# Block pairs in another product order: two products accumulate onto a tile that one ScalarE copy took

## The chip, the cores and the metric

One core of a Trainium2 chip runs the kernel. The metric is the time of one execution on the device in microseconds (us), the median of several runs. TensorE multiplies (PE in the profile), VectorE (DVE) and ScalarE (ACT) do elementwise work, GpSimd (POOL) issues the accumulating DMAs, SyncE (SP) the loads.

## The reference

One layer of a streaming encoder on 576 tokens (512 of a prompt and 64 of a running stream), 1024 channels, all in fp32:

```python
def encoder_layer(x, ...):
    x = x + 0.5 * swiglu_ffn(rms_norm(x, ffn1_norm), ffn1_w_gate_up, ffn1_w_down)
    h = rms_norm(x, mix_norm)
    p = h @ w_in
    ...
    y_b = b_act @ w_b_out
    merged = jax.nn.sigmoid(gate_a) * y_a + jax.nn.sigmoid(gate_b) * y_b
    x = x + merged @ w_out
    x = x + 0.5 * swiglu_ffn(rms_norm(x, ffn2_norm), ffn2_w_gate_up, ffn2_w_down)
    return x, ...

def swiglu_ffn(x, w_gate_up, w_down):
    gate, up = jnp.split(x @ w_gate_up, 2, axis=-1)
    return (jax.nn.silu(gate) * up) @ w_down
```

The hidden width of both FFNs is 2816, which is 22 tiles of 128.

## The kernel before

**Exact products.** Activations and weights are split into a high part, rounded to fp32r, and a low part, the rest. A product is three matmuls: high by high, high by low, low by high. Activations lie with channels on partitions and tokens in the free direction, 576 tokens as two halves of H = 288.

**Block pairs.** Where two output tiles (an FFN's gate and up tile of one index i) read the same activations, the kernel works on a 2 x 2 block form: weight blocks A11, A12, A21, A22 (two tiles by two halves of the 1024 channels) against activation blocks (two halves of channels by two halves of tokens). Instead of eight block products it takes seven, by sums: weight sums s1 = a21 + a22, s2 = s1 + a11, s3 = a11 + a21, s4 = s2 + a12, with signs folded into the arithmetic, and activation sums t1 to t4, made once for a phase (`Forms.operands`). The seven weight blocks of a pair are its *units* 0 to 6, the seven products are numbered in the same way. A product is 12 matmuls (4 tiles of channels by 3) of 128 x 128 weights with 288 columns, and fills one bank of PSUM. PSUM has four tiles of two banks each (`mmps`); `bank()` hands out one bank at a time. There are 41 such pairs: FFN1 i = 4 to 21, FFN2 i = 1 to 21, and two in branch B's output projection (`block_pair`).

**Combining.** In `pair`, after each product a step runs that takes the products so far into `t` (the gate's tile, both halves) and `cu` (the up tile): ScalarE copies product 0 out of PSUM (288 columns), VectorE does six additions up to the end of `gate`, where `t` is multiplied by R (the norm's reciprocal root) and ScalarE takes its Silu. A seventh addition comes later in `up`. `up`, `hidden` (the product of the two, and its high part by ScalarE) and `parts` (the low part) are appended to `rest` and run behind the first products of the next pair, one a product. In the last group of each FFN, `up` holds another multiply by R (`if last`).

**The weight stream.** `Stream` (`ws`) loads raw weights by SyncE and prepares units ahead of their use: `add` makes the sums on VectorE, `begin` casts the high part on ScalarE, `end` subtracts for the low part on VectorE. For units that are raw weights the low part is instead made by ScalarE (times -1) and an accumulating DMA that GpSimd issues (`how == "dma"`). `get(n)` leads the stream on to six units past n (`AHEAD_UNITS`), so the fetch for one product casts a unit that is used a pair later, roughly.

**Order.** Each engine runs its instructions in the order in which the code issues them (`Ordered`). In a pair, the fetch `ws.get(...)` for product n comes ahead of its matmuls, and the step on product n - 1 behind them; so the gate of a pair is issued behind the fetch for product 6. Pairs run in groups of hidden tiles (`GROUPS`: 0 to 4, 5 to 9, 10 to 15, 16 to 21). After each group follow the down products of the group: two output tiles at a time for j = 0, 1 (`both`), then one by one.

Of the kernel before, what the change touches and what calls it, by code (L numbers as in the profile page):

```python
# [13 lines left out]
ALU = mybir.AluOpType  # L14
# [8 lines left out]
KU = KT // 2  # L23
T = SEQ + DSEQ
H = T // 2
# [86 lines left out]
def tile_encoder_step(  # L112
# [237 lines left out]
    def plan_block(name, raws, homes, low="dma"):  # L350

        a21, a22, a11, a12 = raws
        s1, s2, s3, s4 = ((name, n) for n in range(1, 5))
        plan[name] = [
            ws.unit(src, KU, home, how, sums)
            for home, (src, how, sums) in zip(homes, (
                (a11, low, ((s1, (a21, a22)),)),
                (s2, "dve", ((s2, (s1, a11)),)),
                (s1, "dve", ()),
                (s3, "dve", ((s3, (a11, a21)),)),  # L360
                (a12, low, ()),
                (s4, "dve", ((s4, (s2, a12)),)),
                (a22, low, ()),
            ))
        ]
        ws.second.update(plan[name][n] for n in (1, 5, 6))

    def plan_ffn(f, gu, dn):
        for g, grp in enumerate(GROUPS):
# [79 lines left out]
            got += [(w, kk) for kk in range(ws.units[n][1])]  # L449
        return got  # L450

    def block(w, xs):

        q = bank()[:, :H]
        for k in range(KU):
            (whi, wlo), (xh, xl) = w, xs[k]
            for m, (l, r) in enumerate(((whi, xh), (whi, xl), (wlo, xh))):
                pe.matmul(q, l[:, k, :], r, start=k == m == 0, stop=k == KU - 1 and m == 2)
        return q


    work = []
# [180 lines left out]
    class Forms:  # L643
# [25 lines left out]
        def operands(self, xg):  # L669

            first, second = (
                [(half(hi, s), half(lo, s)) for hi, lo in xg] for s in range(2)
            )
            t1, t2, t3, t4 = (
                [(half(hi, s), half(lo, s)) for hi, lo in (self.parts[p][i] for p in range(KU))]
                for i in range(2) for s in range(2)
            )
            return first[:KU], t2, t1, t3, first[KU:], second[KU:], t4


    ss = Sum()
# [138 lines left out]
    def ffn(f, xg, sums, finish, forms, R=None, todo=()):  # L820
# [40 lines left out]
                    step(p)  # L861

        def pair(i, hs, last):
            qu, uu, t, cu = (ttile() for _ in range(4))
            q1, u2, u3, u4 = half(qu, 0), half(qu, 1), half(uu, 0), half(uu, 1)
            q = []

            def q7():
                dve.tensor_tensor(u3, q[3], u2, op=ALU.add)
                dve.tensor_tensor(half(cu, 1), u3, q[2], op=ALU.subtract)  # L870
# [14 lines left out]
            for n, xs in enumerate(bs):  # L885
                q.append(block(ws.get(plan[f, "s", i][n]), xs))
                if n > 0:
                    steps[n - 1]()
                if rest:
                    rest.pop(0)()  # L890

            hs.append(None)
            at = len(hs) - 1

            def up():
                if last:
                    dve.tensor_tensor(t, t, R, op=ALU.mult)
                dve.tensor_tensor(half(cu, 0), q[6], u3, op=ALU.add)

            def hidden():  # L900
                dve.tensor_tensor(cu, cu, t, op=ALU.mult)
# [337 lines left out]

    def block_pair(i):  # L1240
        j = 2 * i
        c1, c2, qu, uu = (ttile() for _ in range(4))
        q1, u2, u3, u4 = half(qu, 0), half(qu, 1), half(uu, 0), half(uu, 1)
        q = []

        def second():
            dve.tensor_tensor(u3, q[3], u2, op=ALU.add)
            dve.tensor_tensor(half(c2, 1), u3, q[2], op=ALU.subtract)

            if i == KU - 1:  # L1250
                MS[4], MS[5] = split(M[4]), split(M[5])

        def first():
            dve.tensor_tensor(half(c1, 1), q[5], u4, op=ALU.add)
            dve.tensor_tensor(c1, c1, SGB[j], op=ALU.mult)
            merged(j, c1)

        steps = (
            lambda: sca.copy(q1, q[0]),
            lambda: dve.tensor_tensor(u2, q[1], q1, op=ALU.subtract),  # L1260
            lambda: dve.tensor_tensor(u4, q[2], u2, op=ALU.subtract),
            second,
            lambda: dve.tensor_tensor(half(c1, 0), q[4], q1, op=ALU.add),
            first,
        )
        for n, xs in enumerate(bs):
            q.append(block(ws.get(plan["yb", "s", i][n]), xs))
            if n > 0:
                steps[n - 1]()
        dve.tensor_tensor(half(c2, 0), q[6], u3, op=ALU.add)  # L1270
        dve.tensor_tensor(c2, c2, SGB[j + 1], op=ALU.mult)
        merged(j + 1, c2)
        spare.clear()
# [164 lines left out]
```

## Time and profile before

| | |
|---|---|
| runs | 1294.07, 1295.1, 1296.71 us, median 1295.1 us |
| profiled execution: span from first to last instruction | 1290.1 us |
| TensorE | 1279.4 us busy, 99%, 9728 matmuls |
| VectorE | 925.1 us, 72%, 1539 instructions |
| ScalarE | 765.5 us, 59%, 1359 instructions |
| GpSimd | 361.6 us, 28%, 460 instructions |

The profiled execution has no time of its own beside its span; the median of the runs lies 5.0 us above it. The profile gives busy time by engine, a chain of waits followed back from the last instruction, a list of what each engine waited for, and a timeline. A timeline row reads: start in us, duration, engine, line, operation, output and inputs by the program's names, shapes, count, and in brackets the idle time before it and what ended it. Neighbouring instructions of one kind are merged into one row, so that 12 matmuls of a product make one. All rows have line 88, since a helper records every operation.

### The profile page before, as it was taken

The page shows a single profiled execution, that of the slowest core. Times are in us where ns is not written, and L with a number is a line of the kernel's source. Part 1 is how long each engine was busy: PE and PEld are TensorE (multiplying, and loading weights), DVE is VectorE, ACT ScalarE, POOL GpSimd, SP SyncE. Part 2 cuts the span into 40 slices and gives each one's busy share as a digit, 9 for nine tenths or more (in the row PEclk, how much of TensorE's full clock was granted, in tenths as well). Part 3 has the DMA queues.
Part 4 walks back from the last instruction along what each step waited for, and adds up shares of the span by engine and source line. Part 5 has one row for each costly group of instructions (what it writes and reads, how often), then busy time and mean ns, then how long its engine had stood idle before and what let it go on. Part 6 is the DMA issues. An engine that isn't in the chain of part 4 may idle for free.

```text
span 1290.1 us, 25702 instructions
## 1 busy us (share of the span) xinstructions
PE 1279.4 (99%) x9728; PEld 1277.5 (99%) x9728; DVE 925.1 (72%) x1539; ACT 765.5 (59%) x1359; POOL 361.6 (28%) x460
## 2 busy tenths in 40 slices
PE   9999999999999999999999999999999999999997
PEld 9999999999999999999999999999999999999997
DVE  6868668748846998888895166656867848847956
ACT  7655646646776645555444576477665655654664
POOL 0032332232333444333321221122142141241230
PEclk9999999999999999999999999999999999999998
DMA  7286787886799898788885767696687696796783
GB/s 220 70 181 154 163 180 155 177 181 149 154 224 232 174 200 173 165 172 174 172 172 124 163 142 154 151 236 145 139 175 171 151 197 151 164 204 138 158 172 97
DMA packets 286812, 215.26 MB, mean 167 GB/s; under 512 B 15456, under 2 KB 248928, under 8 KB 286688
## 3 DMA queue, kind: packets, MB, share of 16 engines
q0 software_dynamic: 56160, 92.43, 43.3%
q1 hardware_dynamic: 228784, 120.35, 32.8%
q8 instruction: 77, 1.26, 0.4%
q10 hardware_dynamic: 1744, 0.83, 0.2%
q14 instruction: 47, 0.39, 0.1%
HBM read 116.17 MB, written 4.98 MB: 94 GB/s over the span
## 4 chain that ended last, share of the span: by engine, by line
PE 92%; issue 4%; DVE 2%; DMA 1%; ACT 1%; POOL 0%; DVEq 0%; POOLq 0%; ACTq 0%
PE mm L88 92%; DVE tmp L88 0%; DMA g<-raw 0%; DMA raw<-in_w_b_out_dram 0%; DVE x L88 0%; DVE g L88 0%; DMA u<-raw 0%; ACT act L88 0%; DVE w L88 0%; POOL u L88 0%; DVE act L88 0%; ACT u L88 0%; ACT w L88 0%; ACT g L88 0%; POOL g L88 0%
## 5 line engine op out<-in xcount | busy, mean ns | idle before, releaser
L88 PE MATMUL mm<-act,u 128*128 128x288 f32 x4758 | 668.3, 293 | 0.1
L88 PEld LDWEIGHTS mm<-act,u 128*128 128x128 f32 x4758 | 638.9, 188 | 0.4 <-DMA u<-raw 0.3
L88 PE MATMUL mm<-act,g 128*128 128x288 f32 x3030 | 432.9, 294 | 0.9 <-DMA g<-raw 0.9
L88 PEld LDWEIGHTS mm<-act,g 128*128 128x128 f32 x3030 | 410.3, 188 | 1.1 <-DMA g<-raw 1.1
L88 POOL DMA_DIRECT2D u<-raw x197 | 172.3, 874 | 481.7 <-ACT u L88 317.4
L88 PE MATMUL mm<-act,act 128*128 128x288 f32 (+2 forms) x1896 | 259.9, 293 | 0.0
L88 PEld LDWEIGHTS mm<-act,act 128*128 128x128 f32 x1896 | 252.2, 188 | 0.5 <-ACT act L88 0.3
L88 ACT CAST u<-raw 128x512 fp32r<-128x512 f32 (+2 forms) x207 | 118.8, 574 | 172.0 <-PE mm L88 136.7
L88 POOL DMA_DIRECT2D g<-raw x126 | 109.9, 872 | 297.4 <-ACT g L88 242.7
L88 DVE SCALAR_TENSOR_TENSOR w<-g,prm,w 128x606 f32<-128x606 f32 x232 | 179.3, 844 | 1.4 <-ACT w L88 1.4
L88 DVE TENSOR_TENSOR tmp<-mm,tmp 128x288 f32<-128x288 f32 (+1 forms) x251 | 112.9, 459 | 70.3 <-PE mm L88 53.7
L88 ACT ACTIVATE u<-u 128x512 fp32r<-128x512 f32 (+2 forms) x197 | 116.8, 593 | 6.2
L88 ACT CAST g<-raw 128x512 fp32r<-128x512 f32 (+2 forms) x136 | 75.1, 553 | 43.9 <-DMA raw<-in_ffn_w_down_dram 17.6
L88 DVE SCALAR_TENSOR_TENSOR tmp<-mm,r 128x576 f32<-128x576 f32 x48 | 36.3, 757 | 76.6 <-PE mm L88 76.6
L88 POOL DMA_DIRECT2D act<-raw x67 | 59.1, 883 | 108.3 <-ACT act L88 94.5
L88 ACT CAST act<-tmp 128x576 fp32r<-128x576 f32 x92 | 61.9, 675 | 43.1 <-DVE tmp L88 42.1
L88 ACT CAST g<-w 128x512 fp32r<-128x512 f32 x79 | 49.0, 620 | 64.4 <-DVE w L88 58.6
L88 ACT CAST u<-w 128x512 fp32r<-128x512 f32 x81 | 50.2, 619 | 61.0 <-DVE w L88 43.6
L88 DVE TENSOR_TENSOR act<-tmp,act 128x576 fp32r<-128x576 f32 x92 | 67.5, 754 | 18.1 <-ACT act L88 16.5
L88 ACT ACTIVATE g<-g 128x512 fp32r<-128x512 f32 (+2 forms) x126 | 72.1, 572 | 4.0
L88 DVE TENSOR_TENSOR w<-raw,raw 128x512 f32<-128x512 f32 x82 | 56.2, 685 | 16.2 <-DMA raw<-in_ffn_w_gate_up_dram 11.2
L88 ACT ACTIVATE tmp<-tmp 128x576 f32<-128x576 f32 x47 | 32.2, 686 | 45.1 <-DVE tmp L88 45.0
(86 smaller groups left out, 830.6 us busy)
## 6 DMA issues: line engine op xcount, KB each, us to landing
raw<-in_ffn_w_gate_up_dram SPq DMA_DIRECT2D x171, 256.0 KB, 3.5
u<-raw POOLq DMA_DIRECT2D x140, 256.0 KB, 4.2
raw<-in_w_in_dram SPq DMA_DIRECT2D x112, 256.0 KB, 3.8
raw<-in_ffn_w_down_dram SPq DMA_DIRECT2D x96, 192.0 KB, 3.8
g<-raw POOLq DMA_DIRECT2D x69, 256.0 KB, 4.2
act<-raw POOLq DMA_DIRECT2D x61, 256.0 KB, 4.4
g<-raw POOLq DMA_DIRECT2D x43, 192.0 KB, 4.5
u<-raw POOLq DMA_DIRECT2D x41, 192.0 KB, 4.5
```

Source lines behind the costliest of these rows:

```text
L88: return self.tc.keep_in_program_order(fn(*args, **kwargs))
```

## The change

A function `seven` takes the place of the loops in `pair` and `block_pair`. It takes two PSUM tiles of two banks (`first`, `second`) and one bank (`last`). Units 1 and 2 trade places, so that products 0 and 1 lie in the two banks of `first`, and one ScalarE copy of 576 columns takes both. Products 4 and 5 are then multiplied with `start=False` onto the same two banks, and so add up with products 0 and 1 in place. After product 3 VectorE does three additions (`middle`). After product 5, ScalarE copies bank 0 as the first half of the gate, VectorE adds for the second half, and the gate follows (`close`). The last addition (product 6) is returned as a function and runs where it ran. A pair then has five additions on VectorE where it had seven, two ScalarE copies where it had one.

```diff
                 (a11, low, ((s1, (a21, a22)),)),
-                (s2, "dve", ((s2, (s1, a11)),)),
-                (s1, "dve", ()),
+                (s1, "dve", ((s2, (s1, a11)),)),
+                (s2, "dve", ()),
                 (s3, "dve", ((s3, (a11, a21)),)),
...
-    def block(w, xs):
+    def block(w, xs, q, new):
-        q = bank()[:, :H]
...
+                pe.matmul(
+                    q, l[:, k, :], r, start=new and k == m == 0,
+                    stop=k == KU - 1 and m == 2, skip_group_check=not new,
+                )
+    def seven(ws7, xs7, c1, c2, gate, between=None):
+        qq, uu = ttile(), ttile()
+        u2, u3 = half(uu, 0), half(uu, 1)
+        first, second = psum2(), psum2()
+        q = [first[:, 0, :H], first[:, 1, :H], second[:, 0, :H], second[:, 1, :H]]
+        def middle():
+            dve.tensor_tensor(u2, q[2], half(qq, 0), op=ALU.subtract)
+            dve.tensor_tensor(u3, q[3], u2, op=ALU.add)
+            dve.tensor_tensor(half(c2, 1), u3, half(qq, 1), op=ALU.subtract)
+        def close():
+            sca.copy(half(c1, 0), q[0])
+            dve.tensor_tensor(half(c1, 1), q[1], u2, op=ALU.subtract)
+            gate()
+        steps = {
+            1: lambda: sca.copy(halves(qq), first[:, :, :H]),
+            3: middle,
+            5: close,
+        }
+        last = bank()[:, :H]
+        for n, (w, xs) in enumerate(zip(ws7, xs7)):
+            block(ws.get(w), xs, (q + q[:2] + [last])[n], n not in (4, 5))
+            if n in steps:
+                steps[n]()
+            if between:
+                between()
+        return lambda: dve.tensor_tensor(half(c2, 0), last, u3, op=ALU.add)
...
         def pair(i, hs, last):
...
             def gate():
-                dve.tensor_tensor(half(t, 1), q[5], u4, op=ALU.add)
                 dve.tensor_tensor(t, t, R, op=ALU.mult)
                 sca.activation(t, t, AF.Silu)
-            steps = (
-                lambda: sca.copy(q1, q[0]),
-                lambda: dve.tensor_tensor(u2, q[1], q1, op=ALU.subtract),
-                lambda: dve.tensor_tensor(u4, q[2], u2, op=ALU.subtract),
-                q7,
-                lambda: dve.tensor_tensor(half(t, 0), q[4], q1, op=ALU.add),
-                gate,
-            )
-            for n, xs in enumerate(bs):
-                q.append(block(ws.get(plan[f, "s", i][n]), xs))
-                if n > 0:
-                    steps[n - 1]()
+            final = seven(plan[f, "s", i], bs, t, cu, gate, between)
```

Before, the step on product 5 stood behind the fetch for product 6; now it stands ahead of it. What this does to the engines' order, at three places:

ScalarE, from the gate of a pair in the last group of FFN1. Before (`tmp_722` is the gate's tile, `g_746` the unit that the fetch for product 6 casts, which is unit 5 of the next pair; `act_762` the high part of the hidden product):

```order
L88 CAST g_746_4252<-w_744_4233 128x512 [waits DVE_49,PE_49]
L88 ACTIVATE tmp_722_4121<-tmp_722_4121 128x576 [waits DVE_49]
L88 CAST u_754_4278<-raw_701_3984 128x512 [waits DMAHW3_49,PE_49]
L88 ACTIVATE u_754_4278<-u_754_4278 128x512 [waits Activation_49]
L88 CAST g_759_4304<-raw_739_4196 128x512 [waits DMAHW0_49,PE_49]
L88 ACTIVATE g_760_4305<-g_759_4304 128x512 [waits DMASW7_49,PE_49,Activation_49]
L88 COPY tmp_749_4271<-mm_748_4255 128x288 [waits DVE_49]
L88 CAST act_762_4324<-tmp_723_4122 128x576 [waits DVE_49]
```

And after (`tmp_734` is the gate's tile, `u_759` the cast of unit 5 of the next pair, `tmp_762` the copy of the next pair's products 0 and 1):

```order
L88 COPY tmp_734_4241<-mm_738_4245 128x288 [waits PE_49]
L88 ACTIVATE tmp_734_4241<-tmp_734_4241 128x576 [waits DVE_49,Activation_49]
L88 CAST u_759_4375<-w_756_4352 128x512 [waits DMASW1_49]
L88 CAST g_768_4399<-raw_718_4110 128x512 [waits DMAHW7_49]
L88 ACTIVATE g_769_4400<-g_768_4399 128x512 [waits DMASW6_49,Activation_49]
L88 CAST u_774_4426<-raw_752_4316 128x512 [waits DMAHW4_49,DMASW2_49,PE_49]
L88 ACTIVATE u_774_4426<-u_774_4426 128x512 [waits Activation_49]
L88 COPY tmp_762_4391<-mm_764_4393 128x576 [waits PE_49]
L88 CAST act_775_4444<-tmp_735_4242 128x576 [waits DVE_49]
```

The Silu (ACTIVATE of the gate's tile, 576 columns) stood behind the cast of unit 5 of the next pair, and now stands ahead of it, behind a copy that is new; the copy of the next pair has 576 columns in place of 288.

VectorE at the same place. Before (the first three rows are the gate's last additions and its multiply by R, `g_747` the low part of unit 5 of the next pair, whose cast is `g_746`; the second multiply by R follows):

```order
L88 TENSOR_TENSOR tmp_722_4121<-mm_743_4217,tmp_720_4119 128x288 [waits PE_49]
L88 TENSOR_TENSOR tmp_722_4121<-mm_743_4217,tmp_721_4120 128x288
L88 TENSOR_TENSOR tmp_722_4121<-tmp_722_4121,r_78_421 128x576 [waits DVE_49]
L88 TENSOR_TENSOR g_747_4253<-w_744_4233,g_746_4252 128x512 [waits DMASW6_49,Activation_49]
L88 TENSOR_TENSOR w_753_4276<-raw_728_4133,raw_729_4135 128x512 [waits DMAHW7_49,DMAHW6_49]
L88 TENSOR_TENSOR tmp_722_4121<-tmp_722_4121,r_78_421 128x576 [waits Activation_49]
L88 TENSOR_TENSOR tmp_723_4122<-mm_748_4255,tmp_721_4120 128x288 [waits PE_49]
L88 TENSOR_TENSOR w_758_4302<-w_753_4276,raw_739_4196 128x512 [waits DMAHW0_49,DVE_49]
L88 TENSOR_TENSOR tmp_723_4122<-tmp_723_4122,tmp_722_4121 128x576 [waits DVE_49]
```

After (the first row is the addition for the second half of the gate, `u_759` the low part of unit 5 of the next pair):

```order
L88 TENSOR_TENSOR tmp_734_4241<-mm_738_4245,tmp_737_4244 128x288 [waits Activation_49]
L88 TENSOR_TENSOR tmp_734_4241<-tmp_734_4241,r_78_421 128x576 [waits DVE_49]
L88 TENSOR_TENSOR u_759_4375<-w_756_4352,u_759_4375 128x512 [waits DMASW1_49,Activation_49]
L88 TENSOR_TENSOR w_767_4397<-raw_743_4256,raw_744_4258 128x512 [waits DMAHW3_49,DMAHW2_49]
L88 TENSOR_TENSOR tmp_734_4241<-tmp_734_4241,r_78_421 128x576
L88 TENSOR_TENSOR tmp_735_4242<-mm_712_4097,tmp_737_4244 128x288 [waits PE_49]
L88 TENSOR_TENSOR w_773_4424<-w_767_4397,raw_752_4316 128x512 [waits DMAHW4_49,DVE_49]
L88 TENSOR_TENSOR tmp_735_4242<-tmp_735_4242,tmp_734_4241 128x576 [waits DVE_49]
L88 TENSOR_TENSOR act_778_4461<-tmp_735_4242,act_775_4444 128x576 [waits Activation_49]
```

The low part still follows the gate's multiply, but it reads a cast which ScalarE now issues behind the Silu of that multiply's result. An addition is gone.

TensorE at the first pair of FFN1, the last matmuls of product 3 and the first of product 4. Before (`mm_175` holds products 2 and 3, `mm_181` is the tile that product 4 takes):

```order
L88 MATMUL mm_175_901<-act_149_825,u_155_837 128x288
L88 MATMUL mm_175_901<-act_144_720,u_155_837 128x288
L88 MATMUL mm_181_939<-act_39_239,g_156_839 128x288 [waits PE_49,Activation_49]
L88 MATMUL mm_181_939<-act_40_240,g_156_839 128x288
L88 MATMUL mm_181_939<-act_39_239,g_157_840 128x288 [waits DVE_49]
```

After (`mm_166` holds products 2 and 3, `mm_165` products 0 and 1):

```order
L88 MATMUL mm_166_857<-act_149_825,u_155_837 128x288
L88 MATMUL mm_166_857<-act_144_720,u_155_837 128x288
L88 MATMUL mm_165_856<-act_39_239,g_156_839 128x288 [waits Activation_49]
L88 MATMUL mm_165_856<-act_40_240,g_156_839 128x288
L88 MATMUL mm_165_856<-act_39_239,g_157_840 128x288 [waits DVE_49]
```

Product 4 went to a tile of its own; it now goes onto the bank of product 0, and its first matmul waits for ScalarE, which is the copy of both banks.

More of the change, by code (lines that the diff above doesn't have):

```diff
@@ L365, in plan_block @@
         ]
-        ws.second.update(plan[name][n] for n in (1, 5, 6))
+        ws.second.update(plan[name][n] for n in (2, 5, 6))
     def plan_ffn(f, gu, dn):
@@ L1241, in block_pair, with between @@
         j = 2 * i
[L1242 to L1251, printed above, removed]
+        c1, c2 = ttile(), ttile()
         def first():
-            dve.tensor_tensor(half(c1, 1), q[5], u4, op=ALU.add)
             dve.tensor_tensor(c1, c1, SGB[j], op=ALU.mult)
             merged(j, c1)
[L1258 to L1270, printed above, removed]
+        def between():
+            if i == KU - 1 and between.n == 4:
+                MS[4], MS[5] = split(M[4]), split(M[5])
+            between.n += 1
+        between.n = 0
+        seven(plan["yb", "s", i], bs, c1, c2, first, between)()
         dve.tensor_tensor(c2, c2, SGB[j + 1], op=ALU.mult)
```

14 lines of the change are left out of this document (4 added, 10 removed).

## The prediction

> **What bounds the kernel now.** I read the page first (engine totals, then the chain), next the list of what TensorE waited for, and then the timeline of each engine over one pair of the last feed-forward group, because its queues are the fullest.
>
> ```profile
> span 1290.1 us, 25702 instructions
> PE 1279.4 (99%) x9728; PEld 1277.5 (99%) x9728; DVE 925.1 (72%) x1539; ACT 765.5 (59%) x1359; POOL 361.6 (28%) x460
> PE 92%; issue 4%; DVE 2%; DMA 1%; ACT 1%; POOL 0%; DVEq 0%; POOLq 0%; ACTq 0%
> ...
> PE mm L88 <- DMA g<-raw: 0.9, 1, 0.9
> PE mm L88 <- ACT tmp L88: 0.5, 1, 0.5
> ```
>
> TensorE is busy for 99% of the span and is 92% of the chain that ended last. After start-up it waited twice for something that this change can touch: 0.9 us for a weight's low part and 0.5 us for ScalarE. Nearly nothing can be won while TensorE keeps the same matmuls; what can be lost is any wait that reaches it. So the question is whether the new dependence (product 4 of a pair waits for a copy by ScalarE) is met in time. Products are numbered 0 to 6, weight units of a pair too, a time with a + counts from the start of product 0 of the pair, and unit 5 and product 5 of the *next* pair are written 5'.
>
> ```profile
> 1219.85 1.74 PE L88 MATMUL mm<-act,u 128*128 128x288 f32 x12
> 1226.16 1.74 PE L88 MATMUL mm<-act,u 128*128 128x288 f32 x12
> 1230.89 1.74 PE L88 MATMUL mm<-act,g 128*128 128x288 f32 x12
> 1241.94 3.33 PE L88 MATMUL mm<-act,u 128*128 128x288 f32 x24
> ```
>
> These rows of TensorE's timeline are product 0 and product 4 of a pair, product 0 of the last pair, and the first down product. A pair takes 1230.89 - 1219.85 = 11.04 us, the last one 1241.94 - 1230.89 = 11.05, a product 1.58, and product 4 starts at +6.31. The two other engines over the same pair:
>
> ```profile
> 1221.33 0.69 ACT L88 ACTIVATE tmp<-tmp 128x576 f32<-128x576 f32 x1 [1.40 <-DVE tmp L88]
> 1221.92 0.60 ACT L88 CAST u<-raw 128x512 fp32r<-128x512 f32 x1
> 1224.27 0.38 ACT L88 COPY tmp<-mm 128x288 f32<-128x288 f32 x1
> 1224.84 0.68 ACT L88 CAST act<-tmp 128x576 fp32r<-128x576 f32 x1 [0.19 <-DVE tmp L88]
> 1225.42 0.61 ACT L88 CAST u<-w 128x512 fp32r<-128x512 f32 x1
> 1225.94 0.62 ACT L88 CAST g<-w 128x512 fp32r<-128x512 f32 x1
> 1232.10 0.69 ACT L88 ACTIVATE tmp<-tmp 128x576 f32<-128x576 f32 x1 [0.86 <-DVE tmp L88]
> ...
> 1220.54 0.76 DVE L88 TENSOR_TENSOR tmp<-tmp,r 128x576 f32<-128x576 f32 x1
> 1221.21 0.69 DVE L88 TENSOR_TENSOR g<-w,g 128x512 fp32r<-128x512 f32 x1
> 1221.82 0.68 DVE L88 TENSOR_TENSOR w<-raw,raw 128x512 f32<-128x512 f32 x1
> 1222.42 0.75 DVE L88 TENSOR_TENSOR tmp<-tmp,r 128x576 f32<-128x576 f32 x1
> 1223.09 0.45 DVE L88 TENSOR_TENSOR tmp<-mm,tmp 128x288 f32<-128x288 f32 x1
> 1223.45 0.68 DVE L88 TENSOR_TENSOR w<-w,raw 128x512 f32<-128x512 f32 x1
> 1224.05 0.75 DVE L88 TENSOR_TENSOR tmp<-tmp,tmp 128x576 f32<-128x576 f32 x1
> 1225.55 0.76 DVE L88 TENSOR_TENSOR act<-tmp,act 128x576 fp32r<-128x576 f32 x1 [0.37 <-ACT act L88]
> 1226.22 0.69 DVE L88 TENSOR_TENSOR u<-w,u 128x512 fp32r<-128x512 f32 x1
> 1226.83 0.69 DVE L88 TENSOR_TENSOR w<-raw,raw 128x512 f32<-128x512 f32 x1
> 1228.39 0.45 DVE L88 TENSOR_TENSOR tmp<-mm,tmp 128x288 f32<-128x288 f32 x1
> 1228.88 0.45 DVE L88 TENSOR_TENSOR tmp<-tmp,mm 128x288 f32<-128x288 f32 x1
> 1229.25 0.68 DVE L88 TENSOR_TENSOR u<-w,u 128x512 fp32r<-128x512 f32 x1
> 1229.85 0.68 DVE L88 TENSOR_TENSOR w<-w,raw 128x512 f32<-128x512 f32 x1
> 1231.31 0.76 DVE L88 TENSOR_TENSOR tmp<-tmp,r 128x576 f32<-128x576 f32 x1
> ```
>
> The reader is to see the gate's multiply (1220.54), the Silu (1221.33), then VectorE's low part at 1221.21, which began before the Silu, since its cast was done. From multiply to multiply the loop takes 1231.31 - 1220.54 = 10.77, a little under a pair of 11.04.
>
> **The change part by part.** *Removed:* two VectorE additions in each of 41 pairs. Instructions of that kind follow each other at 1229.25 - 1228.88 = 0.37, so 82 x 0.37 = 30 us of VectorE. VectorE is 2% of the chain, so most of this buys nothing by itself.
>
> ```profile
> L88 ACT COPY tmp<-mm 128x576 f32<-128x576 f32 x8 | 5.0, 623 | 0.0
> L88 ACT COPY tmp<-mm 128x288 f32<-128x288 f32 x41 | 15.8, 384 | 9.0 <-PE mm L88 9.0
> ```
>
> *Added:* ScalarE's 41 copies grow from 0.384 to 0.623, and 41 copies of 0.384 come in: 41 x 0.239 + 41 x 0.384 = 25.5 us on an engine that is 59% busy. By itself that costs nothing either; it is covered by ScalarE's idle 41%, as long as no one waits for its place in the queue.
>
> *Moved, and this I hold to be the decisive part:* the close of a pair (copy, last addition, gate multiply, Silu) is now issued ahead of the fetch of the last unit, so on ScalarE the Silu stands before the cast of unit 5', and on VectorE the low part of unit 5' stands right behind the gate multiply. That low part needs the cast, the cast waits behind the Silu, the Silu waits for the multiply. All that VectorE has behind it (the next sums, the hidden product, whose high part is again ScalarE's, the middle step, the next close) hangs on that chain. One turn of it, by start differences of the rows above: multiply to Silu 0.79, Silu to cast 0.59, cast 0.62 and 0.03 to land: 2.03. Low 0.61, sum 0.60, second multiply by R 0.67, final addition 0.36, sum 0.60, hidden product until its cast 0.79, that cast until VectorE goes on 0.71: 6.37. Low of the activation 0.67, low 0.61, sum 0.60: 8.25. Middle step 0.49 + 0.49 + 0.37: 9.60. Two lows and a sum, 0.60 each, and the last addition 0.49 (as from 1228.39 to 1228.88): 11.89. TensorE's pair is 11.04: the chain falls behind by 0.85 us a pair, where before it gained 0.27. The second multiply by R is in the last group of each FFN alone; elsewhere the turn is 11.22, at most 0.18 behind, and five turns of that stay within the slack named next.
>
> *The new wait.* In the pair after a group's first, the Silu starts at -1.58 + 0.17 (product 5 out) + 0.41 (copy) + 0.49 + 0.79 = +0.28. From the Silu to the end of the wide copy stand on ScalarE: 0.59 (Silu), 0.52 (cast 5', 1225.42 to 1225.94), four weight casts 1224.27 - 1221.92 = 2.35, the copy 0.62 + 0.03: 4.11. So the copy ends at +4.39, and product 4 needs it at +6.31: slack 1.92. In the last group it ends at 4.39, 5.24, 6.09 in the second to fourth pair, 6.94 in the fifth (wait 0.63), and, that wait having been given back, 7.16 in the sixth (wait 0.85): 1.48 for a group. Ends: 0 if the loop keeps pace, and 5 x 0.85 = 4.3 if it had no slack; I take 1.48, which the row by row sum gives.
>
> *The down product behind it.* The accumulate DMAs of its units are issued behind the same casts.
>
> ```profile
> 1238.00 0.86 POOL L88 DMA_DIRECT2D u<-raw  x1
> ...
> u<-raw POOLq DMA_DIRECT2D x41, 192.0 KB, 4.5
> ```
>
> Before, this issue came 1238.00 - 1232.10 = 5.90 behind the Silu; with cast 5' and the wider copy ahead of it, 5.90 + 0.52 + 0.29 = 6.7. With the Silu at 7.16 - 4.11 = +3.05 in the sixth pair, and 4.5 to land, it is there at +14.26; the product that reads it would want it at 11.05 + 0.85 (the wait) + 0.80 (six matmuls of the first unit) + 0.52 (four more before its low part) = +13.2. Wait 1.05; ends 0 (before, the Silu at +1.21, it was there 0.7 ahead, so a landing 1 us quicker hides it) and 2. A last group costs 1.48 + 1.05 = 2.5, twice 5.0.
>
> *First pairs.* There the copy is late for another reason: ScalarE is still behind with casts.
>
> ```profile
> 63.17 1.74 PE L88 MATMUL mm<-act,g 128*128 128x288 f32 x12
> 914.49 1.74 PE L88 MATMUL mm<-act,g 128*128 128x288 f32 x12
> 928.91 2.08 PE L88 MATMUL mm<-act,u 128*128 128x288 f32 x12
> ...
> 63.41 0.39 ACT L88 COPY tmp<-mm 128x288 f32<-128x288 f32 x1
> 915.19 0.38 ACT L88 COPY tmp<-mm 128x288 f32<-128x288 f32 x1
> ```
>
> Product 4 of FFN1's first pair starts at 63.17, the copy that it will wait for at 63.41: 63.41 + 0.65 - 63.17 = 0.9 of wait. In FFN2's first pair: 915.19 + 0.65 - 914.49 = 1.35. That wait lets VectorE and ScalarE catch up, so the wait that before fell at 928.91 (0.5 by the list of waits) goes; the next pairs have no margin left (0.1), and the down product after that group I put at 0.6, between 0 and the 1.05 of the last group. FFN2's first group: 1.35 - 0.5 + 0.1 + 0.6 = 1.55. The other groups and the two pairs of branch B I put at 0, with 0.5 either way, by the slack of 1.92.
>
> *Sum:* 5.0 + 0.9 + 1.55 = 7.45 on the profiled span of 1290.1: 1297.5. The median of the runs shown, 1295.1, lies 5.0 above that span, so 1302.5.
>
> **A rule weighed.** The trace has the wide copy 1.92 us clear of product 4 in a pair that is not behind. The Trainium skill (Perfetto Trace Analysis, Matmuls under Optimizing Tensor Performance) says that independent matmul groups should rotate through different PSUM banks so that the evacuation of one overlaps the next group's matmuls. Here two products go back to a bank that has just been evacuated, so by that rule every pair is at risk; if each of the 41 lost the last group's mean of 1.48 / 5 = 0.3, the sum would grow to about 12 us, 1307. By the rows two other products lie between, and only a late ScalarE exposes the copy.
>
> **The rivals.** *A, no measurable change (0.2% of 1295.1 is 2.6 us, about what a measurement can tell):* the serial turn is shorter than my 11.89, because an instruction that waits on another engine is picked up sooner than the back to back rows show; from 0.85 us less a turn nothing accumulates. For it: the turn before (10.77) had 0.27 to spare. Against: 0.85 is made of whole instructions, 1.14 of Silu and cast. Then only the first pairs count: 0.9 + 1.35 - 0.5 = 1.75, 1296.9.
>
> *B, faster:* VectorE's relief is what counts. The removed 30 us are 3.3% of its 925.1; of its 2% of the chain (26 us) that is 0.85, and twice this if the additions stood where others wait; with the waits of 0.9 and 0.5 gone too, up to 3.1 us are won, 1292.0. It decides if the turn of the loop ends below 11.04 and the copies of the first pairs, too, come earlier by 0.9 and 1.35, since VectorE holds up ScalarE there. For it: 72% busy VectorE; against: the casts ahead of the copy at 63.41 wait for no VectorE. The rule that the Trainium skill gives in VectorE: DVE Perf Modes, Rules for kernel authors, to minimize the count of operations, speaks for this rival; the chain of this trace speaks against it.
>
> *C, much slower:* the lag is larger (a fifth more, 1.02 a pair), the landings under load take 5.4, and the groups without the second multiply reach the wait in their last pair as well. Then the copies of a last group cost 2.3, its down product 1.9, four other groups 0.7 each: 1290.1 + 0.9 + 1.55 + 8.4 + 2.8 + 5.0 = 1308.8.
>
> **How the numbers follow.** My forecast, slower by stalls in the last groups and the first pairs, gets 0.55, with its own range 1299.5 to 1305.5 from the ends above (down product 0 to 2 in each of two groups, 0.5 for the rest). A gets 0.20, B 0.07, C 0.12, and 0.06 go to a half lag between A and the forecast, on the slow side. Slower by over 0.2%: 0.55 + 0.12 + 0.06 = 0.73; within: 0.20; faster: 0.07. The time is that of the forecast. The range goes down to 1296.0, which takes in most of A, and up to 1308.5, just under the centre of C; outside lie B, half of C and the lower part of A, about 0.2.
>
> **What would show it.** VectorE 82 instructions fewer, ScalarE 41 more. In the list of waits, TensorE waiting for ScalarE's copy: at 63 us, at 914 us, and late in the last groups of the two FFNs, the second from 1180 to 1245 us (I hold FFN1's to be like it); in these, from pair to pair, the Silu 0.85 later against product 0, and VectorE idle before the low part of unit 5' with ScalarE as the releaser. If the Silu keeps its distance, the serial turn is wrong and A or B holds; if TensorE waits at product 4 in groups without the second multiply, C. I'm also wrong if waits fall on the down products for other transfers, or TensorE's step between matmuls changes when two products share a bank.

## The result and the profile after

The changed kernel takes 1303.05 us, the median of seven runs (1298.63 to 1304.42); the kernel before, on the same chip, 1294.64 us (1291.48 to 1296.71, seven runs). The ratio is 1.0061, 95% interval 1.004 to 1.0082: slower by 7.9 us (0.0061 of 1294.64; the two medians lie 8.4 apart), with 1302.5 forecast. A second set of six runs gave 1300.88 us and the ratio 1.0063 (1.004 to 1.0087).

The page of the changed kernel (span and instruction count, busy time by engine, the chain that ended last) and its list of what TensorE waited for (us in total, times, longest):

```profile
span 1302.3 us, 25532 instructions
...
PE 1285.8 (99%) x9728; PEld 1281.7 (98%) x9728; DVE 898.3 (69%) x1457; ACT 785.6 (60%) x1400; POOL 360.5 (28%) x460
...
PE 81%; DVE 7%; issue 6%; ACT 2%; DMA 2%; POOL 1%; DVEq 0%; POOLq 0%; SPq 0%; ACTq 0%
```

```profile
PE mm L88 <- ACT tmp L88: 4.4, 7, 1.2
PE mm L88 <- DMA g<-raw: 1.3, 3, 0.9
...
PE mm L88 <- DMA u<-raw: 0.9, 1, 0.9
```

VectorE has 82 instructions fewer and 27 us less work, and that bought nothing. TensorE's share of the chain fell from 92 to 81%: it waits for ScalarE's copies six times (the seventh wait of that row is the one at the end of the kernel, 0.5 us, which before had too), and VectorE and ScalarE have come into the chain. Where, the timeline of TensorE shows (in brackets idle time and releaser; these are the products 4 and the first down products):

```profile
63.35 1.85 PE L88 MATMUL mm<-act,g 128*128 128x288 f32 x12 [0.73 <-ACT tmp L88]
...
342.52 1.85 PE L88 MATMUL mm<-act,g 128*128 128x288 f32 x12 [0.62 <-ACT tmp L88]
354.24 1.85 PE L88 MATMUL mm<-act,u 128*128 128x288 f32 x12 [0.35 <-ACT tmp L88]
361.49 1.71 PE L88 MATMUL mm<-act,g 128*128 128x288 f32 x11 [0.92 <-DMA g<-raw]
...
923.17 1.85 PE L88 MATMUL mm<-act,g 128*128 128x288 f32 x12 [1.21 <-ACT tmp L88]
...
1235.89 1.85 PE L88 MATMUL mm<-act,u 128*128 128x288 f32 x12 [0.56 <-ACT tmp L88]
1247.63 1.85 PE L88 MATMUL mm<-act,g 128*128 128x288 f32 x12 [0.42 <-ACT tmp L88]
1254.85 1.32 PE L88 MATMUL mm<-act,u 128*128 128x288 f32 x8 [0.90 <-DMA u<-raw]
```

A wait counted from start to start is 0.16 us longer than the bracket, since ends of matmuls are modelled, and the product behind it takes 1.85 in place of 1.74. Both are in the numbers below. ScalarE and VectorE in the last group of FFN2:

```profile
1219.83 0.69 ACT L88 ACTIVATE tmp<-tmp 128x576 f32<-128x576 f32 x1 [2.23 <-DVE tmp L88]
1220.42 0.60 ACT L88 CAST u<-w 128x512 fp32r<-128x512 f32 x1
...
1231.76 0.69 ACT L88 ACTIVATE tmp<-tmp 128x576 f32<-128x576 f32 x1 [2.23 <-DVE tmp L88]
...
1235.22 0.62 ACT L88 COPY tmp<-mm 128x576 f32<-128x576 f32 x1
...
1243.71 0.69 ACT L88 ACTIVATE tmp<-tmp 128x576 f32<-128x576 f32 x1 [2.23 <-DVE tmp L88]
...
1246.95 0.62 ACT L88 COPY tmp<-mm 128x576 f32<-128x576 f32 x1
```

```profile
1218.98 0.76 DVE L88 TENSOR_TENSOR tmp<-tmp,r 128x576 f32<-128x576 f32 x1
1221.06 0.69 DVE L88 TENSOR_TENSOR u<-w,u 128x512 fp32r<-128x512 f32 x1 [1.32 <-ACT u L88]
...
1230.91 0.76 DVE L88 TENSOR_TENSOR tmp<-tmp,r 128x576 f32<-128x576 f32 x1
```

The reader is to see the chain of the forecast: multiply 1218.98, Silu 1219.83, cast 1220.42, and VectorE idle for 1.32 us before the low part that needs that cast. From Silu to Silu it is 11.93 and 11.95 us, from multiply to multiply 11.93, and TensorE's pair is 11.04. The copy ends at 1235.22 + 0.62 = 1235.84, and product 4 starts at 1235.89.

The two profiled spans differ by more, 12.2 us, and the waits account for 7.85 of it: the execution profiled for the changed kernel was one of those in which TensorE's step between 450 and 800 us, where both kernels issue the same work, is 131.5 ns and not 130.0; the last section shows it. The profiled execution of the second set has the step of 130.0 ns, as the kernel before has, and a span of 1297.8 us: with like steps the change costs 7.7 us of span.

### The profile page after: what moved, and what is told of

Read it like the earlier page. It is cut to its first block, busy times and chain, and to the rows that moved or that the text cites. A ratio compares the mean times of both kernels' runs of the same rounds, so it can differ in the third digit from the quotient of the medians.

```text
span 1302.3 us, 25532 instructions
## 1 busy us (share of the span) xinstructions
PE 1285.8 (99%) x9728; PEld 1281.7 (98%) x9728; DVE 898.3 (69%) x1457; ACT 785.6 (60%) x1400; POOL 360.5 (28%) x460
## 3 DMA queue, kind: packets, MB, share of 16 engines
q8 instruction: 76, 1.25, 0.4%
## 4 chain that ended last, share of the span: by engine, by line
PE 81%; DVE 7%; issue 6%; ACT 2%; DMA 2%; POOL 1%; DVEq 0%; POOLq 0%; SPq 0%; ACTq 0%
PE mm L88 81%; DVE tmp L88 3%; DMA g<-raw 1%; DVE w L88 1%; DVE act L88 1%; DVE u L88 1%; DVE g L88 1%; ACT act L88 1%; ACT u L88 1%; ACT tmp L88 0%; ACT g L88 0%; POOL u L88 0%; DMA u<-raw 0%; POOL g L88 0%; DMA raw<-in_ffn_w_gate_up_dram 0%
## 5 line engine op out<-in xcount | busy, mean ns | idle before, releaser
L88 DVE TENSOR_TENSOR tmp<-mm,tmp 128x288 f32<-128x288 f32 (+1 forms) x169 | 78.1, 462 | 30.2 <-ACT tmp L88 19.1
L88 DVE TENSOR_TENSOR u<-w,u 128x512 fp32r<-128x512 f32 x81 | 55.6, 686 | 22.6 <-ACT u L88 22.4
```

Source lines behind the costliest of these rows:

```text
L88: return self.tc.keep_in_program_order(fn(*args, **kwargs))
```

## The experiments

Ratios are to the kernel before, measured beside each, with 95% intervals.

| kernel | us, median | ratio |
|---|---|---|
| changed kernel | 1303.05 | 1.0061 (1.004 to 1.0082) |
| whole close behind the fetch | 1304.5 | 1.0099 (1.0077 to 1.012) |
| first pairs apart | 1301.66 | 1.0073 (1.0049 to 1.0096) |
| no second multiply by R | 1297.21 | 1.0028 (1.0015 to 1.0041) |
| whole close behind the fetch, first pairs apart | 1304.74 | 1.0092 (1.0069 to 1.0116) |
| split close | 1295.51 | 1.0014 (1.0 to 1.0027) |
| split close, FFN1's first pair apart | 1293.43 | 1.0003 (0.9989 to 1.0018) |
| before, gate early | 1332.12 | 1.0301 (1.0279 to 1.0323) |
| before, gate early, product 6 apart | 1303.85 | 1.008 (1.0063 to 1.0098) |
| changed kernel again | 1300.88 | 1.0063 (1.004 to 1.0087) |

**Without the second multiply by R.**

```diff
             def up():
-                if last:
-                    dve.tensor_tensor(t, t, R, op=ALU.mult)
                 final()
```

> The changed kernel without the second multiply by R in the last group of each FFN (12 VectorE multiplies fewer; the hidden product there lacks one factor). Theory: the turn there falls from 11.94 (Silu to Silu as measured) to 11.27, 0.22 behind TensorE's pair in place of 0.9; the copies of the last groups then end by +5.3, ahead of product 4 at +6.31, and their waits go, with 0 to 0.3 us left on the down products: 5 us below the changed kernel, about 1298. Rival (the order of the queues does not matter, the wide copy is late by itself): waits unchanged, 0 won.

ScalarE's Silus in the last group of FFN2, and the list of waits:

```profile
1211.46 0.69 ACT L88 ACTIVATE tmp<-tmp 128x576 f32<-128x576 f32 x1 [1.83 <-DVE tmp L88]
...
1222.73 0.69 ACT L88 ACTIVATE tmp<-tmp 128x576 f32<-128x576 f32 x1 [2.05 <-DVE tmp L88]
```

```profile
PE mm L88 <- ACT tmp L88: 2.5, 3, 1.2
```

The turn is 11.27, as forecast to the hundredth, and the waits of both last groups are gone: of six waits for a copy only those of the two first pairs are left (the third in the row is the one at the end). 0.0033 of the ratio, 4.3 us, went with 12 VectorE instructions of 0.75 us. So the last groups lose their time by the lag; the bank alone costs nothing there, since their products 4 still go onto evacuated banks in this run.

**The whole close behind the fetch for product 6.**

```diff
         for n, (w, xs) in enumerate(zip(ws7, xs7)):
-            block(ws.get(w), xs, (q + q[:2] + [last])[n], n not in (4, 5))
+            got = ws.get(w)
+            if n == 6:
+                close()
+            block(got, xs, (q + q[:2] + [last])[n], n not in (4, 5))
```

(Step 5 is taken out of `steps`.)

> The changed kernel with one difference: the close of a pair is issued behind the fetch for product 6, so that on ScalarE the cast of unit 5 of the next pair stands ahead of the close's copy and the Silu again; VectorE's order and all products stay. Theory (the serial turn Silu, cast, low part): without the 1.36 us of Silu and cast ahead of the low part a turn is 11.89 - 1.36 = 10.53 us, below TensorE's 11.04, so the Silu keeps its distance from pair to pair and the waits for the copy and on the down products in the last groups go (before: 0.88 + 0.62 + 1.18 at 342, 354 and 361 us, 0.82 + 0.69 + 1.17 at 1236, 1248 and 1255 us, with the slower step behind each); the two first pairs keep their 1.0 and 1.5 us. Time 5 to 6.5 us below the changed kernel, about 1297. Rival (a bank just evacuated is the cost, wherever the copy stands): the waits at product 4 in the last groups stay within 0.3 us of what they were, time as the changed kernel, about 1303.

This expectation failed: 1304.5 us, no faster than the changed kernel. ScalarE, VectorE, and the waits:

```profile
1219.04 0.62 ACT L88 CAST u<-w 128x512 fp32r<-128x512 f32 x1 [1.34 <-DVE w L88]
1219.57 0.39 ACT L88 COPY tmp<-mm 128x288 f32<-128x288 f32 x1
1221.34 0.69 ACT L88 ACTIVATE tmp<-tmp 128x576 f32<-128x576 f32 x1 [1.38 <-DVE tmp L88]
...
1233.02 0.69 ACT L88 ACTIVATE tmp<-tmp 128x576 f32<-128x576 f32 x1 [1.38 <-DVE tmp L88]
```

```profile
1219.99 0.46 DVE L88 TENSOR_TENSOR tmp<-mm,tmp 128x288 f32<-128x288 f32 x1 [1.03 <-ACT tmp L88]
```

```profile
PE mm L88 <- DMA g<-raw: 2.9, 5, 0.9
PE mm L88 <- ACT tmp L88: 2.8, 5, 1.2
PE mm L88 <- DMA u<-raw: 2.0, 3, 0.8
```

The low part waits no more, but another hop has come into the turn. The close has an instruction on ScalarE that the old gate hadn't, the copy of bank 0. Now it stands behind the cast of unit 5 of the next pair, that cast waits for a sum on VectorE (1.34), and VectorE's last addition, which writes the other half of the tile that the copy writes, waits for the copy (1.03). The turn is 1233.02 - 1221.34 = 11.68, and 11.66 to 11.69 in the groups without the second multiply too, where the changed kernel had 11.27; so TensorE waited eight times for a weight's low part, in place of four times. What I had overlooked is that a copy is moved with the rest of the close.

**First pairs apart.**

```diff
+        third = psum2() if apart else first
+        q45 = [third[:, 0, :H], third[:, 1, :H]]
         def close():
+            if apart:
+                dve.tensor_tensor(half(qq, 1), half(qq, 1), u2, op=ALU.subtract)
+                dve.tensor_tensor(half(c1, 0), q45[0], half(qq, 0), op=ALU.add)
+                dve.tensor_tensor(half(c1, 1), q45[1], half(qq, 1), op=ALU.add)
+            else:
...
-            block(ws.get(w), xs, (q + q[:2] + [last])[n], n not in (4, 5))
+            block(ws.get(w), xs, (q + q45 + [last])[n], apart or n not in (4, 5))
```

> The changed kernel, but in the first block pair of each FFN products 4 and 5 go to a PSUM tile of their own and VectorE adds them (three additions in place of one addition and one ScalarE copy, in two pairs of 41). Theory: product 4 there waits for no copy, so the waits of 1.0 us at 63 and of 1.5 us at 923 us go; those of the last groups stay. In FFN2's first group up to 0.5 us comes back as in the kernel before, at a later product. Time 2 to 2.5 us below the changed kernel, about 1300.8. Rival (these waits are weights that are late in any case): another wait of the same size takes their place, 0 won.

Product 4 of FFN1's first pair and, in FFN2, product 4 and the one behind it in the *second* pair:

```profile
62.35 1.74 PE L88 MATMUL mm<-act,g 128*128 128x288 f32 x12
...
928.97 2.10 PE L88 MATMUL mm<-act,u 128*128 128x288 f32 x12 [1.84 <-ACT tmp L88]
930.87 3.06 PE L88 MATMUL mm<-act,g 128*128 128x288 f32 x12
```

In FFN1 the theory held: the 1.0 us is gone and nothing took its place. In FFN2 the wait moved on to the next pair, and the copy came 2.0 us late there. VectorE had worked without a pause from 917.79 to 924.80 us, with the two additions more of this edit among it; the Silu behind that had waited 3.18 us, and the copy stands behind the Silu. TensorE's clock fell after that wait (the last section). So the 1.5 us does not hang on the first pair's bank: it is the backlog of VectorE and ScalarE, paid at the next product that waits for a copy. Both are needed, since the kernel before, where no product 4 waits for a copy, paid 0.5 us for its backlog. How much of the 2.0 us comes from the two additions more was not separated. With both edits (whole close and first pairs apart) neither repaired the other:

> The changed kernel with both: the close behind the fetch for product 6, and the first pairs' products 4 and 5 in a tile of their own. Theory: all waits that the change brought go, 8 to 8.5 us below the changed kernel, within 1 us of the kernel before, about 1294.5; VectorE's 78 instructions fewer buy nothing. Rival (VectorE's relief counts once the waits are gone): 2 us or more below the kernel before, 1292.5.

It gave 1304.74 us; the lag of the late close was there as before, and so was FFN2's moved wait, 1.5 us at 936 us.

**The split close.** The copy is issued right behind product 5, the rest of the close behind the fetch.

```diff
         def close():
-            sca.copy(half(c1, 0), q[0])
             dve.tensor_tensor(half(c1, 1), q[1], u2, op=ALU.subtract)
             gate()
         steps = {
             1: lambda: sca.copy(halves(qq), first[:, :, :H]),
             3: middle,
-            5: close,
+            5: lambda: sca.copy(half(c1, 0), q[0]),
         }
...
-            block(ws.get(w), xs, (q + q[:2] + [last])[n], n not in (4, 5))
+            got = ws.get(w)
+            if n == 6:
+                close()
+            block(got, xs, (q + q[:2] + [last])[n], n not in (4, 5))
```

> The changed kernel with the close split: ScalarE's copy of 288 columns is issued right behind product 5, and the last addition, the multiply by R and the Silu behind the fetch for product 6. ScalarE then has copy, cast of unit 5 of the next pair, Silu. The run with the whole close behind the fetch had a turn of 11.67 us (Silu to Silu), because its copy stood behind the cast, the cast behind a VectorE sum, and VectorE's last addition waited 1.03 us for the copy. Theory (both hops make the lag): with neither, the turn falls to 11.67 - 1.14 = 10.53 if nothing else held it up, under TensorE's 11.04, so no lag: Silu to Silu 11.04 to 11.1 in all groups, the waits in the groups after the first pairs go (0.3 at 254, 2.8 in each last group, 0.5 at 963 us), 6.4 us less than the changed kernel; the first pairs' waits of 1.0 and 1.5 stay. Time about 1296.5. Rival (accumulating onto an evacuated bank costs by itself): lag or waits at product 4 in the last groups stay, 1302 or more.

```profile
1210.20 0.69 ACT L88 ACTIVATE tmp<-tmp 128x576 f32<-128x576 f32 x1 [0.86 <-DVE tmp L88]
...
1219.53 0.40 ACT L88 COPY tmp<-mm 128x288 f32<-128x288 f32 x1 [1.25 <-PE mm L88]
1219.82 0.62 ACT L88 CAST g<-w 128x512 fp32r<-128x512 f32 x1
1221.30 0.69 ACT L88 ACTIVATE tmp<-tmp 128x576 f32<-128x576 f32 x1 [0.86 <-DVE tmp L88]
```

```profile
PE mm L88 <- ACT tmp L88: 2.1, 3, 1.2
...
PE mm L88 <- DMA g<-raw: 0.4, 1, 0.4
```

The copy now waits for TensorE itself (1.25), and Silu to Silu is 11.10, TensorE's own pace: its pair takes 1219.32 - 1208.22 = 11.10 there. The turn of 10.53 that was expected, were nothing else to hold it up, shows in FFN2's first group alone, where the engines catch up: its Silus at 923.17, 933.70 and 944.24 us lie 10.53 and 10.54 apart. Every wait behind the first pairs that came with the change is gone, with all 41 pairs still accumulating onto evacuated banks. 0.0047 of the ratio, 6.1 us, hung on where three instructions of a pair stand.

**Split close, FFN1's first pair apart.** The split close and the `apart` form above, for FFN1's first pair alone.

> The kernel with the split close, and in FFN1's first pair products 4 and 5 in a PSUM tile of their own (three additions on VectorE there). Theory: 1.0 us less than the split close alone; left over the kernel before are the 1.5 us at FFN2's first pair less its 0.5 there, and 0.6 less at 846: within 1 us of the kernel before, about 1295.0. Rival (VectorE's relief is worth something once no wait hides it): 2 us or more below the kernel before.

```profile
PE mm L88 <- ACT tmp L88: 1.7, 2, 1.2
```

1293.43 us, ratio 1.0003 (0.9989 to 1.0018): the kernel before, to within what can be measured, with 80 VectorE instructions fewer. This is the best version of the change that I found, and it doesn't beat the kernel before: the relief of VectorE is worth nothing, with no wait left to hide it but the one of 1.5 us at FFN2's first pair (1.2 in this list; the other is at the end). That wait is no handicap against the kernel before, which has one of about the same size at 846 us (1.0 from start to start, against 1.4 here).

**The order alone, on the old kernel.**

```diff
             for n, xs in enumerate(bs):
+                if n == 6:
+                    steps[5]()
                 q.append(block(ws.get(plan[f, "s", i][n]), xs))
-                if n > 0:
+                if 0 < n < 6:
                     steps[n - 1]()
```

> The kernel BEFORE (old products, no accumulation, no wide copy) with one thing of the change: the gate step of a feed-forward pair (last addition, multiply by R, Silu) is issued ahead of the fetch for product 6. Theory (the serial turn alone does the harm): the low part of unit 5 of the next pair then waits for multiply, Silu and cast, 1.36 us more a turn: Silu to Silu 10.77 + 1.36 = 12.13 in the last groups and 11.46 in the others; product 4 waits for no copy, so the lag comes out on the down products behind the groups, 3 to 4 us for a last group and 0 to 0.5 for another: 6 to 9 us more than the kernel before, about 1302. Rival (only product 4's wait for the copy costs): as the kernel before, 1294.5.

```profile
PE mm L88 <- DVE tmp L88: 27.9, 18, 3.8
```

```profile
118.18 1.74 PE L88 MATMUL mm<-act,u 128*128 128x288 f32 x12
121.52 1.81 PE L88 MATMUL mm<-act,g 128*128 128x288 f32 x12 [1.60 <-DVE tmp L88]
```

```profile
120.56 0.81 DVE L88 TENSOR_TENSOR tmp<-mm,tmp 128x288 f32<-128x288 f32 x2
```

Much slower than expected, for a reason that neither theory had. Products 5 (118.18) and 6 (121.52) share a PSUM tile in every second pair of the old kernel. With the gate's addition issued ahead of product 6, product 6 waits until VectorE has read product 5, which it does with the two additions of 120.56. The expected turn can't be judged by the time of this run, so the run was made again with one line more at the head of `pair`, which gives product 6 a tile of its own:

```diff
             q = []
+            spare.clear()
```

> The kernel BEFORE with the gate step ahead of the fetch for product 6, as in the run that took 1332 us, and with product 6 always in a PSUM tile of its own. In that run TensorE waited 1.9 to 2.4 us at product 6 of every second pair, where products 5 and 6 share a PSUM tile: with the gate's addition issued ahead of product 6, product 6 waits until VectorE has read product 5. Theory: without the shared tile these waits (12 of them, 25 us, and the smaller ones behind the groups) go, and what is left is the serial turn: Silu to Silu 12.13 in the last groups, 11.46 in the others, coming out on the down products behind the groups: 6 to 9 us above the kernel before, about 1301. Rival 1 (a bank read late is what costs, also for other products): waits on VectorE stay, 1315 or more. Rival 2 (the order does no harm without accumulation): as the kernel before, 1293.

```profile
1207.75 0.69 ACT L88 ACTIVATE tmp<-tmp 128x576 f32<-128x576 f32 x1 [2.69 <-DVE tmp L88]
...
1219.87 0.69 ACT L88 ACTIVATE tmp<-tmp 128x576 f32<-128x576 f32 x1 [2.69 <-DVE tmp L88]
```

```profile
1221.10 0.69 DVE L88 TENSOR_TENSOR u<-w,u 128x512 fp32r<-128x512 f32 x1 [1.26 <-ACT u L88]
```

```profile
1255.23 3.65 PE L88 MATMUL mm<-act,u 128*128 128x288 f32 x26 [2.17 <-DMA u<-raw]
```

The turn is 12.12, with 12.13 expected, and nearly the same idle time stands before the low part (1.26 us, 1.32 in the changed kernel). No product 4 waits for a copy here. The lag comes out on low parts that an accumulating DMA makes: most of it on the down products behind the groups (2.17 us in the last one), some already on products ahead of them, such as 0.88 us on product 6 of the last pair of FFN1's last group. The ratio is 1.008 (1.0063 to 1.0098), a little above the 6 to 9 us expected. So the place of the gate in the queues, without accumulation and without a wide copy, is enough for a loss of the size of the whole change's. It falls at other places, so the two sums need not agree.

**The changed kernel again.**

> The changed kernel once more, on the chip of the other three. All theories: about 1303; the waits of its first profile (TensorE 4.4 us for ScalarE's copy, 2.2 us for weights' low parts) come again to 0.3 us. The step of TensorE between two matmuls from 400 to 830 us was 130.0 ns in the profiles of the kernel before and of two others and 131.7 in that of the changed kernel and of a third: if it comes from the kernel it is 131.7 again, if from the execution it may be either.

1300.88 us, ratio 1.0063. The waits came again at the same places. Those for the copies in the last groups were the same to 0.03 us; the one at FFN1's first pair was 0.4 shorter, the ones on transfers changed by up to 0.4, either way. What it says on TensorE's step stands in the last section.

## Why the prediction was right, point by point

| term, us | forecast | measured |
|---|---|---|
| FFN1's first pair, product 4 | 0.9 | 1.0 |
| last groups, products 4 | 1.48 and 1.48 | 1.6 and 1.6 |
| last groups, down product | 1.05 and 1.05 | 1.2 and 1.2 |
| FFN2's first pair, less the waits that it replaces | 1.35 - 0.5 | 1.5 - 0.5 |
| FFN2's first group, other pairs and down product | 0.7 | 0.6 |
| other groups | 0 | 0.3 |
| weight wait at 846 us | not in the sum | -0.65 |
| sum (forecast: a last group's 1.48 + 1.05 rounded to 2.5) | 7.45 | 7.85 |

- **The serial turn** is what the prediction said: forecast 11.89 with the second multiply and 11.22 without, measured 11.94 and 11.27. The runs without the multiply and with the order alone each moved the turn by the amount that the start differences of the old rows give, the split close took it below TensorE's pair, and the waits went and came with it. The whole close moved late did not do what the same sum said (10.53 expected, 11.68 measured), because the place of the copy had been left out of the sum. Rival A is out: instructions that wait on another engine are picked up no sooner.
- **The turn before** was read as 10.77, a gain of 0.27 on TensorE in each pair. That is every second turn only. The turn shown in the prediction begins behind an addition that had waited for TensorE:

```profile
1220.05 0.46 DVE L88 TENSOR_TENSOR tmp<-mm,tmp 128x288 f32<-128x288 f32 x1 [0.46 <-PE mm L88]
```

  It takes in product 5 of the pair before, which in every second pair shares a PSUM tile with product 6, and it starts when product 6 ends (1218.27 + 1.74 = 1220.01). The Silus behind it are at 1221.33, 1232.10 and 1243.42 us, 10.77 and 11.32 apart, on average a pair of TensorE. The old loop had 0.27 to spare, but it gained nothing from pair to pair. The forecast did not rest on it.
- **Products 4 in the last groups.** The two waits are 0.78 and 0.51 (342 and 354 us, start to start, without the slower step) where 0.63 and 0.85 were forecast. The first is larger by 0.15, as much as the turn's 0.05 more makes in the three turns from the second pair to the fifth. The second is smaller, for the most part because I left out of it that the casts ahead of the sixth pair's copy belong to down units, in part of 384 columns: Silu to copy is 3.24 there (1243.71 to 1246.95) against 3.46 a pair earlier. So 1.29 stands against 1.48, and that the table has 1.6 comes from the slower step, 0.1 behind each of the two waits and at the pair before them, whose copy came just in time. The agreement is in part luck.
- **A small term that was missing:** the first matmul or so behind each wait costs 0.1 us more, 1.3 us over the kernel. Taken with the terms, it more than makes up for the weight wait at 846 us, which I had left alone and which was 0.65 shorter. That one moves between executions: it was 0.5 in the first profile of the changed kernel (at 853 us there) and 0.1 in the second.
- **A row misread:** I put the 0.5 us that the list of waits of before has for ScalarE to the product at 928.91. It lies at the end of the kernel:

```profile
1281.21 0.73 PE L88 MATMUL mm<-tmp,ones_r 128*128 128x272 f32 x2 [0.54 <-ACT tmp L88]
```

  What goes at 928.91 shows only in that product's 2.08 us in place of 1.74, and with 0.1 at the pair's first product (at 919.24) makes 0.46, so that the sum came out the same by chance. The list of waits for that window alone names none.
- **First pairs.** Both sizes are right to 0.15 us, the slower step counted in. That FFN2's wait stands for a backlog was said of the wait that it replaced; that it would only move to the next pair if taken away was not, and the run showed it.
- **VectorE's relief (rival B)** is worth nothing that can be measured: ratio 1.0003 with all but one of the waits removed. The op-count rule of the Trainium skill that spoke for it (VectorE: DVE Perf Modes, Rules for kernel authors) finds no support here, where VectorE was 72% busy and not the bound.
- **Banks.** The rule of the Trainium skill on rotating PSUM banks (Perfetto Trace Analysis, Matmuls under Optimizing Tensor Performance) speaks of independent matmul groups; read broadly it would have put every pair at risk. With the split close 39 of the 41 pairs go back to evacuated banks without a wait for it; only where ScalarE is behind does it bite. The trace decides against the broad reading.
- **From the span to the runs,** I added the 5.0 us that the median of before lay above its profiled span. Only 1.7 of that lies around the span (1304.04 us for the profiled execution of the changed kernel, whose span is 1302.3); the rest is the difference between executions, below. Since the sum was made as a difference, it did no harm.

## What to carry to other kernels

Before an edit moves a step ahead of a fetch or behind it, list every instruction that the step issues, engine by engine, and follow one turn of the loop through the queues by start differences of the trace; a turn that is longer than the bound engine's period by 0.9 us cost nothing in the first pairs here, as long as the 1.9 us of slack lasted, and then all of it. A result that two engines write into one tile, or a copy put first in a step, is a hop in that turn like any other. And fewer instructions on an engine with idle time are no gain by themselves: look at what the edit does to their order first.

## What the runs showed of the hardware that was not expected

**TensorE's step has two values, by execution.** One window, 450 to 800 us, of before, of the changed kernel, and of the changed kernel again (span of the window, then busy us and instructions of PE, PEld, DVE, ACT and POOL, granted clock, DMA share, GB/s):

```profile
450.00:800.00 350.00, 350.00 (x2692) 350.00 (x2691) 263.44 (x409) 189.68 (x310) 108.13 (x155) 1.00 0.79 165
```

```profile
450.00:800.00 350.00, 350.00 (x2662) 350.00 (x2661) 259.87 (x401) 185.47 (x304) 107.87 (x156) 1.00 0.79 167
```

```profile
450.00:800.00 350.00, 350.00 (x2692) 350.00 (x2691) 263.80 (x409) 188.76 (x308) 108.66 (x156) 1.00 0.79 167
```

TensorE never waits there and the granted clock is 1.00 in all three, yet it starts 2692 matmuls in one execution and 2662 in another of the same kernel: 350 us over their number is 130.0 ns a step in the one and 131.5 in the other. Over the whole span this makes some 4.5 us (spans of 1297.8 and 1302.3 for the changed kernel), more than half of what the change costs. The two executions run side by side up to 401.6 us, and by 822 us all of the 4.5 us has come in; before and behind that stretch their steps are alike. What sets it stays open; a single profiled span of this kernel should not be compared with another before this window is.

**A wait of 2 us can halve the clock, after the wait.** In the run with the first pairs apart, the product behind the wait at 928.97 ran at full pace up to its last two matmuls, and the next one took 3.06 us in place of 1.74, with a granted clock of 0.66 over these 5 us (the number ahead of DMA's share):

```profile
929.00:934.00 5.00, 5.00 (x26) 5.00 (x27) 4.19 (x8) 3.52 (x7) 1.05 (x3) 0.66 0.85 170
```

For 14 matmuls, some 3.4 us, the step was 240 ns, 1.5 us lost. The kernel with the early gate has twelve waits of 1.9 to 2.4 us (start to start). Eleven of them had no such sequel; the one at 1230.46 us had, 13 matmuls at 240 ns:

```profile
1230.46 2.01 PE L88 MATMUL mm<-act,g 128*128 128x288 f32 x12 [2.06 <-DVE tmp L88]
1232.26 3.08 PE L88 MATMUL mm<-act,u 128*128 128x288 f32 x12
```

In the same run a wait of 4.1 us at 950.32 was followed at once by 19 such matmuls. The Trainium skill (TensorE: Matmul & The Clock Gate, Part 1: The HAM clock gate) tells of a free-running window of about 3.4 us after whose idleness the clock falls to half. The length agrees, with two slow stretches of 3.3 and 3.4 us, and so does the half, with a granted clock of 0.50 from 1232.0 to 1235.2 us in the kernel with the early gate. What differs is that TensorE stood still for only 2.0 and 2.2 us before these two. That other waits of that length had no sequel would fit a window in which the place of the wait counts; no run here shows where the windows lie.
